# A diffusion layer's latents and context laid out turned by the host, and their reciprocal roots computed on all partitions

## The chip, the cores and the metric

The kernel runs on 1 core of a Trainium2 chip, in one launch. The metric is the device time of one execution in microseconds (us), median of several runs.

Engines are named as in the profile: PE is TensorE (PEld its weight loads), DVE is VectorE, ACT is ScalarE, POOL is GpSimd, SP is SyncE, which here only issues DMAs.

## The reference

One layer of a diffusion backbone over 1024 latent tokens of width 1024, with 256 context tokens. What matters for this change is the very first step, the modulated RMS norm of the latents and of the context:

```python
def rms_norm(x, g):
    xf = x.astype(jnp.float32)
    y = xf * lax.rsqrt(jnp.mean(xf * xf, axis=-1, keepdims=True) + EPS)
    return (y * g.astype(jnp.float32)).astype(x.dtype)
...
    m_lat = sc @ w_mod[l] + b_mod[l]
    m_ctx = scc @ w_mod[l] + b_mod[l]
    ...
    h_lat = rms_norm(x, norm1_g[l]) * (1.0 + sc1) + sh1
    h_ctx = rms_norm(ctx, norm1_g[l]) * (1.0 + csc1) + csh1
    y_lat, y_ctx = token_mixers(h_lat, h_ctx, w_in[l], ...)   # h @ w_in: seven blocks of 512 columns, then retention and differential attention
    x = x + g1 * y_lat
    h2 = rms_norm(x, norm2_g[l]) * (1.0 + sc2) + sh2
    x = x + g2 * conv_ffn(h2, w_up[l], conv_w[l], conv_b[l], w_down[l])
return rms_norm(x, final_g)
```

The products of `h_lat` and `h_ctx` with `w_in` contract over the width, so TensorE needs `h` with the width on the partitions. The mean of squares runs over the same width.

## The kernel before, in words

Every large product is made of three passes over operands split into a rounded high part and a low part (fp32r): high by high, high by low, low by high.

The opening of the kernel works on the latents in two halves of 512 tokens (`xs0`, `xs1`: four tiles of 128 tokens x 1024 each) and on the context in two tiles (`xc`). Tokens lie on the partitions. For each tile:

- `square` (line 542, ACT) sums the squares along the row into one column of `sm`.
- `power` takes the reciprocal root: a DVE multiply and add (line 113), then POOL's `pow` with the exponent -0.5 (line 114), both on 128x1.
- `scale` (line 548, DVE) multiplies the row by it.
- `modulate` then turns four 128x128 pieces on PE (line 554, `ident` is the identity), ACT forms the high part `hT[0]` from PSUM with scale and shift of the modulation (line 557), DVE forms the same unrounded as `tmp` (line 559), and DVE or POOL subtracts to get the low part `hT[1]` (line 561). It runs once for each of the 8 pieces `d` of the width.

The modulation columns `mcol` come from `w_mod` beside it: `mod_load` (DMA), `mod_part` (PE, line 526), `mod_row` (ACT, line 530), `mod_sums` (PE line 536, DVE lines 537 and 538).

`part_products(ts, k)` are the first real products: the block of `w_in` that gives the values of the differential attention, for latent tiles 0 and 1, then 2 and 3, over the contraction piece k = 0 to 7 (lines 598, 600, 604). After the loop over k, tiles 4 and 5 follow with `between(t, k)` after each k (lines 131 to 133 of `passes`), and after this stage tiles 6 and 7 and then the two context tiles by `natural`. From there on `pl` products follow.

`turn_over(n)` are products of ones with ones that nobody reads (line 608).

The order of the stage is written out by hand: `in_order(begin)` makes each of PE, DVE, ACT and SP keep the order in which the instructions stand in the program. POOL is not in that list, but its instructions are issued in the order of the program too. So an instruction that waits holds up all that stands behind it on its engine.

`mhalf` is a 128x32 tile of -0.5, `ones` a 128x128 tile of 1. Pools `ev` and `xp` hold the buffers that the changed code uses.

Of the kernel before, what the change touches and what calls it, by code (L numbers as in the profile page):

```python
# [8 lines left out]
F32 = mybir.dt.float32  # L9
# [13 lines left out]
LC = 256  # L23
NTC = LC // P
LK = LC + L
NKT = LK // P
# [41 lines left out]
def r32(ap):  # L68
    return ap.bitcast(F32)
# [3 lines left out]
def kernel(  # L73
    ctx: ExitStack,
    tc: tile.TileContext,
    x: bass.AP,
    ctxt: bass.AP,
    cols: bass.AP,
# [75 lines left out]
    with ExitStack() as p1:  # L154
# [20 lines left out]
        hT = [[hp.tile([P, KD, 512], F32R, name=f"hT{a}{i}") for i in range(2)] for a in range(2)]  # L175
        xs0 = [xr.tile([P, D], F32, name=f"xs{t}") for t in range(4)]
        cT = []
        sm = hp.tile([P, 16], F32, name="sm")
        mcol = hp.tile([P, KD, 2, 2], F32, name="mcol")
# [331 lines left out]
        with ExitStack() as p0:  # L511
# [27 lines left out]

            def square(xt, col):  # L540
                sq = xp.tile([P, D], BF16, name="sq", bufs=1)
                nc.scalar.activation(sq, xt, AF.Square, accum_out=sm[:, col : col + 1])

            def power(col):
                rsqrt(sm[:, col : col + 1], sm[:, col : col + 1], 1.0 / D, EPS, 1)

            def scale(xt, col, c0=0, c1=D):
                nc.vector.tensor_scalar(out=xt[:, c0:c1], in0=xt[:, c0:c1], scalar1=sm[:, col : col + 1], scalar2=None, op0=ALU.mult)

            def modulate(tiles, d, who, hi, lo):  # L550
                n = len(tiles) * P
                pt = pst.tile([P, 512], F32, name="pt", tag="tr")
                for i, t in enumerate(tiles):
                    nc.tensor.transpose(pt[:, i * P : (i + 1) * P], t[:, d * P : (d + 1) * P], ident)
                sh = mcol[:, d, 0, who : who + 1]
                a = mcol[:, d, 1, who : who + 1]
                nc.scalar.activation(hi, pt[:, :n], AF.Identity, scale=a, bias=sh)
                tmp = xp.tile([P, 512], F32, name="tmp", bufs=2)
                nc.vector.tensor_scalar(out=tmp[:, :n], in0=pt[:, :n], scalar1=a, scalar2=sh, op0=ALU.mult, op1=ALU.add)
                eng = nc.gpsimd if d % 2 and d > 1 else nc.vector  # L560
                eng.tensor_tensor(out=lo, in0=tmp[:, :n], in1=r32(hi), op=ALU.subtract)

            mods, wts, rws = mm_tile("pr").rearrange("p (a b) -> p a b", a=2), {}, {}
            part = [mm_tile("pn") for _ in range(4)]
            sl, raws, xc = [], [], []
            xs1 = [xp.tile([P, D], F32, name=f"xs1_{t}") for t in range(4)]

# [17 lines left out]

            def load_row(t, eng=nc.sync):
                eng.dma_start(out=(xs0 + xs1)[t], in_=x[t * P : (t + 1) * P, :])

            def latents(half, d, t0=0, t1=4):
                modulate((xs0, xs1)[half][t0:t1], d, 0, hT[0][half][:, d, t0 * P : t1 * P], hT[1][half][:, d, t0 * P : t1 * P])  # L590

            def context(d):
                modulate(xc, d, 1, cT[0][:, d, :], cT[1][:, d, :])

            def part_products(ts, k):
                hi, lo = wget(k, 0, 512)
                for t in ts:
                    mm(part[t], lat_lhs(t, k)[0], hi, start=(k == 0), stop=False)
                for t in ts:
                    mm(part[t], lat_lhs(t, k)[0], lo, start=False, stop=False)  # L600
                if k == 0 and 3 in ts:
                    latents(0, 1)
                for t in ts:
                    mm(part[t], lat_lhs(t, k)[1], hi, start=False, stop=(k == KD - 1))

            def turn_over(n):
                for _ in range(n):
                    mm(part[3][:, :P], ones, ones, start=True, stop=True)

            store = store_to(dv_row, c0=NTC)  # L610
            begin = len(nc.cur_bb.bb.instructions)
            mod_load(0, 0, nc.scalar)
            load_row(0, nc.scalar)
            w_load(0, 0, 1, nc.scalar)
            nc.sync.dma_start(out=ident, in_=consts[:, K_ID : K_ID + P])
            load_row(1)
            mod_load(0, 1)
            for t in range(2, 4):
                load_row(t)
            for q in range(2):  # L620
# [5 lines left out]
            nc.vector.tensor_copy(cz[:, :, 0:2], csil)  # L626
            turn_over(9)
            mod_part(0, 0)
            mod_load(2, 1)
            turn_over(9)  # L630
            mod_part(0, 1)
            w_load(1)
            turn_over(2)
            nc.vector.tensor_tensor(out=fold, in0=ident[:, 0:2], in1=ident[:, 32:34], op=ALU.add)
            for g in (64, 96):
                nc.vector.tensor_tensor(out=fold, in0=fold, in1=ident[:, g : g + 2], op=ALU.add)
            square(xs0[0], 2)
            power(2)
            scale(xs0[0], 2, 0, 3 * P)
            square(xs0[1], 3)  # L640
            power(3)
            mod_row(0)
            w_split(0, 1, nc.scalar)
            scale(xs0[1], 3, 0, 3 * P)
            mod_sums(0)
            turn_over(1)
            w_split(0, 1, nc.vector)
            square(xs0[2], 4)
            latents(0, 0, 0, 2)
            square(xs0[3], 5)  # L650
            power(4)
            scale(xs0[0], 2, 3 * P, D)
            power(5)
            scale(xs0[1], 3, 3 * P, D)
            scale(xs0[2], 4, 0, 3 * P)
            scale(xs0[3], 5, 0, 3 * P)
            for q in range(2):
                mod_load(3, q)
            for k in range(KD):
                part_products((0, 1), k)  # L660
                if k == 0:
                    for q in range(2):
                        mod_part(1, q)
                    mod_row(1)
                    latents(0, 0, 2, 4)
                    mod_sums(1)
                    w_split(1, 2)
                if k == 1:
                    mod_sums(2)
                    latents(0, 2)  # L670
                    for t in (2, 3):
                        scale(xs0[t], 2 + t, 3 * P, D)
                    for q in range(2):
                        mod_part(3, q)
                    mod_row(3)
                if k == 4:
                    square(xs1[2], 8)
                    power(8)
                    scale(xs1[0], 6)
                if k == 5:  # L680
                    scale(xs1[2], 8)
                    scale(xs1[3], 9)
                if k >= 6:
                    latents(1, 4 * (k - 6))
                    latents(1, 4 * (k - 6) + 1)
                if 0 < k < 5:
                    load_row(k + 3)
                n = k + 4
# [17 lines left out]
                if k in (0, 2, 4):  # L706
                    w_split()
                if k == 3:
                    square(xs1[0], 6)
                    square(xs1[1], 7)  # L710
                    power(6)
                    power(7)
                if k == 4:
                    scale(xs1[1], 7)
                    square(xs1[3], 9)
                    power(9)
                if k == 5:
                    first.close()
                    cp = pctx.enter_context(tc.tile_pool(name="cp", bufs=1, side="right"))
                    cT.extend(cp.tile([P, KD, LC], F32R, name=f"cT{a}") for a in range(2))  # L720
                    for t in range(NTC):
                        xc.append(xp.tile([P, D], F32, name="xc", tag="wt", bufs=5))
                        nc.sync.dma_start(out=xc[t], in_=ctxt[t * P : (t + 1) * P, :])
                if k >= 6:
                    latents(1, 4 * (k - 6) + 2)
                    latents(1, 4 * (k - 6) + 3)
            rtab = load_rope(1)
            for t in range(2):
                store(t, part[t])

            def between(t, k):
                if (t, k) == (4, 1):
                    for i in (2, 3):
                        store(i, part[i])
                if t == 4 and k in (3, 5):
                    i = (k - 3) // 2
                    square(xc[i], i)
                    power(i)
                if t == 4 and k in (5, 7):
                    i = (k - 5) // 2  # L740
                    scale(xc[i], i)
                if t == 5 and k % 2:
                    context(k - 1)
                    context(k)

# [844 lines left out]
def lay_out(inputs):  # L1590
# [16 lines left out]
    def kmajor(w, nb):  # L1607
# [8 lines left out]
        "x": a["x"][0],  # L1616
        "ctxt": a["ctx"][0],
        "cols": cols,
# [25 lines left out]
```

## Time and profile before

| | |
|---|---|
| median of 3 runs | 1389.49 us (1388.88 to 1389.71) |
| profiled execution | 1387.15 us, of which the span is 1385.4 us |
| mean granted TensorE clock | 0.998 |
| PE busy | 1363.2 us, 98% of the span |
| DVE, ACT, POOL busy | 994.4, 732.2, 303.6 us |

The span is what the profiler saw between the first and the last instruction. In lists by line or tile, a row gives the engine, the operation, the tiles written and read (`out<-in`), shapes, the count and then durations; three numbers with strokes are the least, the median and the most in ns. In a timeline a row begins with its start and its length in us; a product of plain f32 stands there as two records.

### The profile page before, as it was taken

To read this page: it belongs to the slowest core of one execution; us is meant where nothing else is said; L and a number is where in the kernel's file an instruction comes from. 1 tells how busy PE (TensorE), PEld (TensorE's weight loads), DVE (VectorE), ACT (ScalarE), POOL (GpSimd) and SP (SyncE) were. 2 spreads that over 40 slices of the span, in tenths; PEclk is the share of its full clock that TensorE was granted. 3 is DMA by queue.
4 is the path that set the end of the run, shared out by engine and by line. 5 is a ranking of instruction groups with operands and counts; after the bars stand their busy time and mean duration, and the time that the engine had idled before them with its cause. 6 is when DMAs were issued, how large, how long until landed. Compare 5 with 4: busy or idle time off the path is not lost. (4 is left out here: it accounts for less than half of the span.)

```text
span 1385.4 us, 19442 instructions
## 1 busy us (share of the span) xinstructions
PE 1363.2 (98%) x7042; PEld 1146.0 (83%) x7042; DVE 994.4 (72%) x1469; ACT 732.2 (53%) x1395; POOL 303.6 (22%) x323
## 2 busy tenths in 40 slices
PE   8999999999999999999999999999999999999997
PEld 6788888888988799998888788888888888888886
DVE  4655773424676898895458997788778877798757
ACT  4652322434675789987136654555545555454543
POOL 1310000002655424411200643222332220000001
PEclk9999999999999999999999999999999999999999
DMA  9546885454565778622410232332323325963523
GB/s 373 202 168 210 296 267 184 145 176 144 155 188 151 208 179 182 139 48 99 172 65 23 99 115 99 114 114 94 112 101 112 113 71 174 373 227 106 175 92 129
DMA packets 94759, 214.61 MB, mean 155 GB/s; under 512 B 9220, under 2 KB 29188, under 8 KB 94152
## 3 DMA queue, kind: packets, MB, share of 16 engines
q1 hardware_dynamic: 85928, 186.90, 39.2%
q0 software_dynamic: 8160, 24.91, 7.9%
q10 hardware_dynamic: 576, 1.57, 0.3%
q8 instruction: 55, 0.90, 0.3%
q14 instruction: 40, 0.33, 0.1%
HBM read 158.03 MB, written 55.31 MB: 154 GB/s over the span
## 5 line engine op out<-in xcount | busy, mean ns | idle before, releaser
L131 PE MATMUL pl<-hT,whi 128*128 128x512 f32 x256 | 105.8, 413 | 0.0
L131 PE MATMUL chain<-T,whi 128*128 128x512 f32 x264 | 103.0, 391 | 1.2 <-ACT ub L1298 0.9
L132 PE MATMUL chain<-T,whi 128*128 128x512 f32 x264 | 102.8, 389 | 0.0
L133 PE MATMUL chain<-T,wlo 128*128 128x512 f32 x264 | 102.4, 389 | 0.0
L133 PE MATMUL pl<-hT,wlo 128*128 128x512 f32 x256 | 100.2, 391 | 0.0
L132 PE MATMUL pl<-hT,whi 128*128 128x512 f32 x256 | 99.9, 390 | 0.0
L876 DVE TENSOR_REDUCE mt<-pA 128x1 f32<-128x1280 f32 x64 | 95.1, 1489 | 3.0 <-PE pA L873 1.3
L873 PE MATMUL pA<-ks,qhl 128*128 128x512 f32 (+1 forms) x384 | 89.5, 369 | 1.4 <-DMA ks<-dk 1.0
L131 PE MATMUL c<-whi,ghl 128*128 128x512 f32 x232 | 90.2, 389 | 0.0
L132 PE MATMUL c<-wlo,ghl 128*128 128x512 f32 x232 | 90.2, 389 | 0.0
L133 PE MATMUL c<-whi,ghl 128*128 128x512 f32 x232 | 90.2, 389 | 0.0
L880 ACT ACTIVATE p<-pA,mt 128x1280 f32<-128x1280 f32 x64 | 85.5, 1336 | 5.5 <-DVE mt L876 5.4
L1044 ACT CAST whi<-cmb 128x512 fp32r<-128x512 f32 x62 | 38.5, 623 | 80.5 <-PE chain L132 66.3
L873 PEld LDWEIGHTS pA<-ks,qhl 128*128 128x128 f32 x384 | 67.7, 189 | 13.8 <-issue 1.4
L905 PE MATMUL pv<-va,aT 128*128 128x128 f32 x640 | 77.0, 275 | 0.1
L1204 POOL TENSOR_TENSOR cmb<-wrb 128x512 f32<-128x512 f32 x19 | 28.3, 1488 | 221.1 <-DMA wrb<-w_up 168.2
L1047 DVE TENSOR_TENSOR wlo<-cmb,whi 128x512 fp32r<-128x512 f32 x62 | 60.0, 970 | 20.4 <-ACT whi L1044 20.4
L905 PEld LDWEIGHTS pv<-va,aT 128*128 128x128 f32 x640 | 73.9, 192 | 0.7 <-DVE yT L934 0.3
L1044 ACT CAST whi<-wra 128x512 fp32r<-128x512 f32 x55 | 33.9, 623 | 72.9 <-PE third L132 42.3
L133 PE MATMUL third<-yT,wlo 128*128 128x512 f32 x168 | 65.4, 389 | 0.0
L132 PE MATMUL third<-yT,whi 128*128 128x512 f32 x168 | 65.4, 389 | 0.0
L131 PE MATMUL third<-yT,whi 128*128 128x512 f32 x168 | 65.4, 389 | 0.0
(327 smaller groups left out, 3843.0 us busy)
## 6 DMA issues: line engine op xcount, KB each, us to landing
wm<-w_mod SPq DMA_DIRECT2D x32, 512.0 KB, 5.1
raw<-w_in SPq DMA_DIRECT2D x27, 512.0 KB, 4.7
wra<-w_up SPq DMA_DIRECT2D x24, 512.0 KB, 3.3
wrb<-w_up SPq DMA_DIRECT2D x22, 512.0 KB, 3.5
W<-w_down SPq DMA_DIRECT2D x44, 256.0 KB, 5.8
ad<-s SPq DMA_DIRECT2D x20, 512.0 KB, 3.6
wra<-ad SPq DMA_DIRECT2D x20, 512.0 KB, 3.7
kvs<-kvg SPq DMA_DIRECT2D x36, 256.0 KB, 3.1
```

The source lines that it names most:

```text
L131: mm(ps, lh, rh, start=first, stop=False, skip_group_check=more)
L132: mm(ps, lh, rl, start=False, stop=False, skip_group_check=more)
L133: return mm(ps, ll, rh, start=False, stop=last, skip_group_check=more)
L873: mm(self.pa[m][:, c0:c1], self.q[:, m, i, qs], self.k[:, m, c0:c1], start=(i == 0), stop=(i == 1))
L876: nc.vector.tensor_reduce(out=self.mt[:, m : m + 1], in_=self.pa[m][:, :LK], axis=AX.X, op=ALU.min)
L880: nc.scalar.activation(self.p[m], self.pa[m][:, :LK], AF.Exp, scale=-1.0, bias=self.mt[:, m : m + 1], accum_out=self.s[:, m : m + 1])
L905: mm(self.pv, self.aT[:, c, :], self.v[:, c, :], start=(c == 0), stop=(c == NKT - 1))
L1044: cast = nc.scalar.copy(hi, src)
L1047: nc.vector.tensor_tensor(out=lo, in0=src, in1=r32(hi), op=ALU.subtract)
L1204: nc.gpsimd.tensor_tensor(out=s1, in0=b1, in1=b2, op=ALU.add)
```

## The change

The host turns x and the context: the new input `xt` holds, for each of five groups of 256 tokens (four of latents, the fifth the context), the width on the partitions as [128, 8, 256]. The context no longer comes as an input of its own.

```diff
-        xs0 = [xr.tile([P, D], F32, name=f"xs{t}") for t in range(4)]
+        xh = [xr.tile([P, 2, KD, GQ], F32, name="xh0")]        # GQ = 256
...
+            def x_load(g, i, eng=nc.sync):
+                dst = xc[i] if g == 4 else xh[g // 2][:, g % 2, 4 * i : 4 * i + 4, :]
+                eng.dma_start(out=dst, in_=xt[g][:, 4 * i : 4 * i + 4, :])
+
+            def squares(g, k0, k1):
+                ...
+                nc.scalar.activation(sqs[g, i][:, k0 % 4 : k0 % 4 + k1 - k0, :], src, AF.Square)
+
+            def summed(g, i):
+                ...
+                nc.vector.tensor_reduce(out=sums[g][:, i, :], in_=sqs[g, i].rearrange("p k q -> p q k"), axis=AX.X, op=ALU.add)
+
+            def over_rows(g, srcs, first, last):
+                if first:
+                    tot[g] = pst.tile([P, GQ], F32, name="ss", tag="tr")
+                for n, src in enumerate(srcs):
+                    mm(tot[g], ones, src, start=first and n == 0, stop=last and n == len(srcs) - 1)
+
+            def rstd(g):
+                r = Rc if g == 4 else R[g // 2][:, g % 2, :]
+                nc.vector.tensor_scalar(out=r, in0=tot[g], scalar1=1.0 / D, scalar2=EPS, op0=ALU.mult, op1=ALU.add)
+                nc.gpsimd.tensor_tensor(out=r, in0=r, in1=mhalf[:, 0:1].to_broadcast([P, GQ]), op=ALU.pow)
+
+            def modulate(src, r, d, who, hi, lo):
+                n = hi.shape[-1]
                 sh = mcol[:, d, 0, who : who + 1]
                 a = mcol[:, d, 1, who : who + 1]
-                nc.scalar.activation(hi, pt[:, :n], AF.Identity, scale=a, bias=sh)
-                tmp = xp.tile([P, 512], F32, name="tmp", bufs=2)
-                nc.vector.tensor_scalar(out=tmp[:, :n], in0=pt[:, :n], scalar1=a, scalar2=sh, op0=ALU.mult, op1=ALU.add)
-                eng = nc.gpsimd if d % 2 and d > 1 else nc.vector
-                eng.tensor_tensor(out=lo, in0=tmp[:, :n], in1=r32(hi), op=ALU.subtract)
+                u = xp.tile([P, 512], F32, name="u", bufs=2)[:, :n]
+                nc.vector.scalar_tensor_tensor(out=u..., in0=src, scalar=a, in1=r, op0=ALU.mult, op1=ALU.mult)
+                nc.scalar.activation(hi, u, AF.Identity, bias=sh)
+                nc.vector.scalar_tensor_tensor(out=lo, in0=u, scalar=sh, in1=r32(hi), op0=ALU.add, op1=ALU.subtract)
+
+            def latents(half, d, g0=0, g1=2): ...      # modulate for groups g0 to g1 of a half
+            def context(d): ...                        # modulate for the context, with Rc
+            def first_latents(): ...                   # piece 0 of group 0: u = x * R on DVE, then hi on ACT, u and lo on DVE
```

The order of the stage, new lines marked (loads of weights and modulations left out):

```diff
+            x_load(0, 1, nc.scalar)
             mod_load(0, 0, nc.scalar)
+            x_load(0, 0)
             ...
+            turn_over(11)
+            for k in (0, 2, 4, 6):
+                squares(0, k, k + 2)
+            for k in (0, 2, 4):
+                over_rows(0, [sqs[0, k // 4][:, k % 4 + e, :] for e in range(2)], k == 0, False)
             mod_part(0, 0)
+            over_rows(0, [sqs[0, 1][:, 2 + e, :] for e in range(2)], False, True)
+            mod_part(0, 1)
             ...
+            rstd(0)
+            opening = first_latents()
+            next(opening)
             mod_row(0)
             w_split(0, 1, nc.scalar)
+            turn_over(1)
             mod_sums(0)
+            next(opening)
             w_split(0, 1, nc.vector)
             ...
             for k in range(KD):
                 part_products((0, 1), k)
                 if k == 0:
+                    for e in range(0, KD, 2):
+                        squares(1, e, e + 2)
+                    for i in range(2):
+                        over_rows(1, [sqs[1, i][:, e, :] for e in range(4)], i == 0, i == 1)
                     for q in range(2):
                         mod_part(1, q)
+                    rstd(1)
+                    latents(0, 0, 1, 2)
                     mod_row(1)
                     mod_sums(1)
                     w_split(1, 2)
+                    latents(0, 1)
                 ...
                 if k == 4:
+                    squares(2, 0, 4)
+                    summed(2, 0)
                 if k == 5:
+                    over_rows(2, [sums[2][:, i, :] for i in range(2)], True, True)
+                    rstd(2)
+                if k == 7:
+                    squares(3, 4, 8)
+                    summed(3, 0)
                 if k >= 6:
+                    latents(1, 3 * k - 16, 0, 1)
+                    if k == 7:
+                        summed(3, 1)
+                    latents(1, 3 * k - 15, 0, 1)
                 ...
                 part_products((2, 3), k)
                 ...
                 if k == 4:
+                    squares(2, 4, 8)
+                    summed(2, 1)
                 if k == 5:
                     ...
+                    latents(1, 0, 0, 1)
+                    latents(1, 1, 0, 1)
                 if k >= 6:
+                    latents(1, 3 * k - 14, 0, 1)
+                if k == 6:
+                    squares(3, 0, 4)
...
+            over_rows(3, [sums[3][:, i, :] for i in range(2)], True, True)
+            rstd(3)
             def between(t, k):
                 ...
+                if t == 4:
+                    latents(1, k, 1, 2)
+                    if k in (3, 5):
+                        squares(4, 2 * k - 6, 2 * k - 2)
+                    if k == 7:
+                        for i in range(2):
+                            summed(4, i)
+                if t == 5:
+                    if k == 0:
+                        over_rows(4, [sums[4][:, i, :] for i in range(2)], True, True)
+                        rstd(4)
+                    else:
+                        context(k - 1)
+                    if k == 7:
+                        context(k)
...
-        "ctxt": a["ctx"][0],
+        "xt": np.concatenate([a["x"][0], a["ctx"][0]]).T.reshape(KD, P, -1, GQ).transpose(2, 1, 0, 3),
```

Gone are `square`, `power`, `scale`, the old `modulate` with its turns, and `load_row`.

More of the change, by code (lines that the diff above doesn't have):

```diff
@@ L24 @@
 NTC = LC // P
+GQ = 256
 LK = LC + L
@@ L76 @@
     x: bass.AP,
-    ctxt: bass.AP,
+    xt: bass.AP,
     cols: bass.AP,
@@ L175 @@
         hT = [[hp.tile([P, KD, 512], F32R, name=f"hT{a}{i}") for i in range(2)] for a in range(2)]
-        xs0 = [xr.tile([P, D], F32, name=f"xs{t}") for t in range(4)]
+        xh = [xr.tile([P, 2, KD, GQ], F32, name="xh0")]
         cT = []
-        sm = hp.tile([P, 16], F32, name="sm")
+        pad(hp, 64)
         mcol = hp.tile([P, KD, 2, 2], F32, name="mcol")
@@ L538, in mod_sums @@
                 nc.vector.tensor_scalar(out=mcol[:, d, 0, :], in0=pm[:, 0, :], scalar1=cl[:, COL_BMOD + d : COL_BMOD + d + 1], scalar2=None, op0=ALU.add)
[L540 to L554, printed above, removed]
+            def x_load(g, i, eng=nc.sync):
+                dst = xc[i] if g == 4 else xh[g // 2][:, g % 2, 4 * i : 4 * i + 4, :]
+                eng.dma_start(out=dst, in_=xt[g][:, 4 * i : 4 * i + 4, :])
@@ new lines, in squares @@
+            def squares(g, k0, k1):
+                i = k0 // 4
+                if k0 % 4 == 0:
+                    sqs[g, i] = ev.tile([P, 4, GQ], F32, name="sq", tag="xhl")
+                src = xc[i][:, k0 % 4 : k0 % 4 + k1 - k0, :] if g == 4 else xh[g // 2][:, g % 2, k0:k1, :]
+                nc.scalar.activation(sqs[g, i][:, k0 % 4 : k0 % 4 + k1 - k0, :], src, AF.Square)
+            def summed(g, i):
+                if i == 0:
+                    sums[g] = ev.tile([P, 2, GQ], F32, name="sqk", tag="xb")
+                nc.vector.tensor_reduce(out=sums[g][:, i, :], in_=sqs[g, i].rearrange("p k q -> p q k"), axis=AX.X, op=ALU.add)
@@ L561, in modulate, with latents @@
-                eng.tensor_tensor(out=lo, in0=tmp[:, :n], in1=r32(hi), op=ALU.subtract)
+                u = xp.tile([P, 512], F32, name="u", bufs=2)[:, :n]
+                nc.vector.scalar_tensor_tensor(out=u.rearrange("p (g q) -> p g q", q=GQ), in0=src, scalar=a, in1=r, op0=ALU.mult, op1=ALU.mult)
+                nc.scalar.activation(hi, u, AF.Identity, bias=sh)
+                nc.vector.scalar_tensor_tensor(out=lo, in0=u, scalar=sh, in1=r32(hi), op0=ALU.add, op1=ALU.subtract)
+            def latents(half, d, g0=0, g1=2):
+                c = slice(g0 * GQ, g1 * GQ)
+                modulate(xh[half][:, g0:g1, d, :], R[half][:, g0:g1, :], d, 0, hT[0][half][:, d, c], hT[1][half][:, d, c])
@@ new lines, in context, with first_latents @@
+            def context(d):
+                modulate(xc[d // 4][:, d % 4 : d % 4 + 1, :], Rc.unsqueeze(1), d, 1, cT[0][:, d, :], cT[1][:, d, :])
+            def first_latents():
+                sh = mcol[:, 0, 0, 0:1]
+                a = mcol[:, 0, 1, 0:1]
+                hi, lo = (hT[i][0][:, 0, 0:GQ] for i in range(2))
+                u = xp.tile([P, 512], F32, name="u", bufs=2)[:, :GQ]
+                nc.vector.tensor_tensor(out=u, in0=xh[0][:, 0, 0, :], in1=R[0][:, 0, :], op=ALU.mult)
+                yield
+                nc.scalar.activation(hi, u, AF.Identity, scale=a, bias=sh)
+                nc.vector.tensor_scalar(out=u, in0=u, scalar1=a, scalar2=sh, op0=ALU.mult, op1=ALU.add)
+                nc.vector.tensor_tensor(out=lo, in0=u, in1=r32(hi), op=ALU.subtract)
+                yield
@@ L565 @@
             sl, raws, xc = [], [], []
-            xs1 = [xp.tile([P, D], F32, name=f"xs1_{t}") for t in range(4)]
+            xh.append(xp.tile([P, 2, KD, GQ], F32, name="xh1"))
+            R = [xp.tile([P, 2, GQ], F32, name=f"R{i}") for i in range(2)]
+            Rc = xp.tile([P, GQ], F32, name="Rc")
+            sqs, sums, tot = {}, {}, {}
             def wget(k, c0, c1):
@@ L584, in w_split @@
                     nc.vector.tensor_tensor(out=lo, in0=raw, in1=r32(hi), op=ALU.subtract)
[L586 to L593, printed above, removed]
             def part_products(ts, k):
@@ L600, in part_products @@
                     mm(part[t], lat_lhs(t, k)[0], lo, start=False, stop=False)
-                if k == 0 and 3 in ts:
-                    latents(0, 1)
                 for t in ts:
@@ L611 @@
             begin = len(nc.cur_bb.bb.instructions)
+            x_load(0, 1, nc.scalar)
             mod_load(0, 0, nc.scalar)
-            load_row(0, nc.scalar)
-            w_load(0, 0, 1, nc.scalar)
+            x_load(0, 0)
+            mod_load(0, 1)
             nc.sync.dma_start(out=ident, in_=consts[:, K_ID : K_ID + P])
[L616 to L619, printed above, removed]
+            w_load(0, 0, 1)
+            for i in range(2):
+                x_load(1, i)
             for q in range(2):
@@ L626 @@
             nc.vector.tensor_copy(cz[:, :, 0:2], csil)
-            turn_over(9)
+            turn_over(11)
[3 more added lines that the diff above has]
+                over_rows(0, [sqs[0, k // 4][:, k % 4 + e, :] for e in range(2)], k == 0, False)
             mod_part(0, 0)
+            over_rows(0, [sqs[0, 1][:, 2 + e, :] for e in range(2)], False, True)
+            mod_part(0, 1)
             mod_load(2, 1)
-            turn_over(9)
-            mod_part(0, 1)
             w_load(1)
-            turn_over(2)
             nc.vector.tensor_tensor(out=fold, in0=ident[:, 0:2], in1=ident[:, 32:34], op=ALU.add)
@@ L636 @@
                 nc.vector.tensor_tensor(out=fold, in0=fold, in1=ident[:, g : g + 2], op=ALU.add)
[L637 to L641, printed above, removed]
+            rstd(0)
+            opening = first_latents()
+            next(opening)
             mod_row(0)
             w_split(0, 1, nc.scalar)
-            scale(xs0[1], 3, 0, 3 * P)
+            turn_over(1)
             mod_sums(0)
-            turn_over(1)
+            next(opening)
             w_split(0, 1, nc.vector)
[L648 to L656, printed above, removed]
             for q in range(2):
@@ L661 @@
                 if k == 0:
+                    for e in range(0, KD, 2):
+                        squares(1, e, e + 2)
+                    for i in range(2):
+                        over_rows(1, [sqs[1, i][:, e, :] for e in range(4)], i == 0, i == 1)
                     for q in range(2):
                         mod_part(1, q)
+                    rstd(1)
+                    latents(0, 0, 1, 2)
                     mod_row(1)
-                    latents(0, 0, 2, 4)
                     mod_sums(1)
                     w_split(1, 2)
+                    latents(0, 1)
                 if k == 1:
@@ L670 @@
                     latents(0, 2)
-                    for t in (2, 3):
-                        scale(xs0[t], 2 + t, 3 * P, D)
                     for q in range(2):
@@ L676 @@
                 if k == 4:
-                    square(xs1[2], 8)
-                    power(8)
-                    scale(xs1[0], 6)
+                    squares(2, 0, 4)
+                    summed(2, 0)
                 if k == 5:
-                    scale(xs1[2], 8)
-                    scale(xs1[3], 9)
+                    over_rows(2, [sums[2][:, i, :] for i in range(2)], True, True)
[3 more added lines that the diff above has]
+                    summed(3, 0)
                 if k >= 6:
-                    latents(1, 4 * (k - 6))
-                    latents(1, 4 * (k - 6) + 1)
+                    latents(1, 3 * k - 16, 0, 1)
+                    if k == 7:
+                        summed(3, 1)
+                    latents(1, 3 * k - 15, 0, 1)
                 if 0 < k < 5:
-                    load_row(k + 3)
+                    x_load(2 + (k - 1) // 2, (k - 1) % 2)
                 n = k + 4
@@ L707 @@
                     w_split()
[L708 to L712, printed above, removed]
                 if k == 4:
-                    scale(xs1[1], 7)
-                    square(xs1[3], 9)
-                    power(9)
+                    squares(2, 4, 8)
+                    summed(2, 1)
                 if k == 5:
@@ L720 @@
                     cT.extend(cp.tile([P, KD, LC], F32R, name=f"cT{a}") for a in range(2))
-                    for t in range(NTC):
-                        xc.append(xp.tile([P, D], F32, name="xc", tag="wt", bufs=5))
-                        nc.sync.dma_start(out=xc[t], in_=ctxt[t * P : (t + 1) * P, :])
+                    for i in range(2):
+                        xc.append(xp.tile([P, 4, GQ], F32, name="xc", tag="wt", bufs=5))
+                        x_load(4, i)
+                    latents(1, 0, 0, 1)
+                    latents(1, 1, 0, 1)
                 if k >= 6:
-                    latents(1, 4 * (k - 6) + 2)
-                    latents(1, 4 * (k - 6) + 3)
+                    latents(1, 3 * k - 14, 0, 1)
+                if k == 6:
+                    squares(3, 0, 4)
             rtab = load_rope(1)
@@ L734, in between @@
                         store(i, part[i])
[L735 to L744, printed above, removed]
+                if t == 4:
[3 more added lines that the diff above has]
+                    if k == 7:
+                        for i in range(2):
+                            summed(4, i)
[7 more added lines that the diff above has]
+                        context(k)
             for t in (4, 5):
```

## The prediction

> **What bounds the kernel now.** I read the engines' totals first, then the table by stage of the opening, which is all that the diff touches.
>
> ```profile
> span 1385.4 us, 19442 instructions
> PE 1363.2 (98%) x7042; PEld 1146.0 (83%) x7042; DVE 994.4 (72%) x1469; ACT 732.2 (53%) x1395; POOL 303.6 (22%) x323
> ...
> 0.00:13.50 13.50, 8.79 (x65) 7.31 (x65) 3.40 (x18) 6.25 (x12) 1.63 (x7) 1.00 0.85 312
> 13.50:58.30 44.80, 42.54 (x297) 30.13 (x298) 30.79 (x59) 22.59 (x37) 9.52 (x10) 1.00 0.82 322
> 58.30:82.10 23.80, 23.80 (x114) 19.33 (x113) 13.73 (x28) 13.80 (x24) 8.37 (x10) 1.00 0.23 87
> 82.10:93.00 10.90, 10.90 (x50) 9.01 (x48) 6.77 (x35) 6.00 (x21) 0.00 (x0) 1.00 0.73 290
> ```
>
> Columns after the length are busy us of PE, PEld, DVE, ACT, POOL. PE is full from 13.5 us on but for 2.3 us, so the end moves by whatever moves PE's stream. The timeline gives the marks that I compare with:
>
> ```profile
> 13.50 0.73 PE L598 MATMUL pn<-whi,hT 128*128 128x512 f32 x2 [0.87 <-ACT hT L557]
> 17.56 0.73 PE L598 MATMUL pn<-whi,hT 128*128 128x512 f32 x2 [0.18 <-ACT hT L557]
> 42.65 0.74 PE L598 MATMUL pn<-whi,hT 128*128 128x512 f32 x2
> 58.34 0.47 PE L131 MATMUL pn<-whi,hT 128*128 128x512 f32 x1
> 82.34 0.39 PE L131 MATMUL pn<-whi,cT 128*128 128x512 f32 x1
> 93.22 0.39 PE L131 MATMUL pl<-hT,whi 128*128 128x512 f32 x1
> ```
>
> They are: first product (k = 0, tiles 0 and 1); k = 0, tiles 2 and 3; start of k = 5; tile 4; context; the first product after all that the diff touches. The context's 48 products take 93.22 - 82.34 = 10.88 us, 0.227 each. The forecast is the new time of the last mark.
>
> **The price that decides: pow on 256 columns.** Before, POOL raised one column at a time, in one place four:
>
> ```profile
> L114 POOL TENSOR_TENSOR sm<-sm,mhalf x18: 550/555/1043, 8.8 to 744.5; 128x1 f32<-128x1 f32 x18
> L273 POOL TENSOR_TENSOR ss<-ss,mhalf x16: 1011/1017/1483, 340.8 to 434.6; 128x4 f32<-128x4 f32 x16
> ...
> 340.81 1.02 POOL L273 TENSOR_TENSOR ss<-ss,mhalf 128x4 f32<-128x4 f32 x1 [1.33 <-ACT ss L272]
> 341.86 1.14 DVE L278 SCALAR_TENSOR_TENSOR o<-o,ss,gn 128x128 f32<-128x128 f32 x4 [1.27 <-POOL ss L273]
> ...
> L916 POOL TENSOR_TENSOR e<-sa 128x1 f32<-128x1 f32 x32 | 6.0, 192 | 0.2
> L561 POOL TENSOR_TENSOR hT<-tmp,hT 128x512 fp32r<-128x512 f32 x6 | 7.7, 1292 | 31.6 <-DVE tmp L559 31.6
> L561 POOL TENSOR_TENSOR cT<-tmp,cT 128x256 fp32r<-128x256 f32 x3 | 2.2, 737 | 7.4 <-DVE tmp L559 7.4
> ```
>
> The page calls POOL's spans rough, but the reader of the four columns starts 0.03 us after the shown end, so this length is real. Three more columns cost 1017 - 555 = 462 ns, 154 ns each, while a subtraction costs (1292 - 737) / 256 = 2.2 ns per column. At 154 ns a pow of 256 columns takes X = 0.555 + 255 x 0.154 = 39.8 us, and there are five (four latent groups and the context). No row shows more than 4 columns. The bounds: from below the subtraction's 2.2 ns, X = 1.1 us; from above the longest four columns, (1483 - 555) / 3 = 309 ns, X = 79 us. That one is a straggler (the median of 16 lies 6 ns above the least), so the range ends lower, at a fifth over the median. I take 154 ns: same operation, engine and type, medians of 34 executions. That work has been replicated 128-fold (every partition raises the same numbers) does not help, since the columns are what costs.
>
> By the Trainium skill (GPSIMD Engine Reference, § 3.1) a two-input elementwise instruction there costs about 2.6 cycles per element of a row at 1.2 GHz. The subtraction's row agrees (2.2 ns); the pow rows do not. By that rule each pow would be an estimate of about 1 us and the sum that of the first rival. The same page's § 2.1 describes the instruction as a loop over the elements in which each core serves its 16 partitions, which is what a cost by the column looks like.
>
> **The other prices.**
>
> ```profile
> 7.35 1.06 ACT L542 ACTIVATE sq<-xs 128x1024 bf16<-128x1024 f32 x1 [1.99 <-DMA xs<-x]
> ...
> L582 ACT CAST whi<-raw x5: 610/1052/1058, 11.3 to 44.1; 128x1024 fp32r<-128x1024 f32 x3, 128x512 fp32r<-128x512 f32 x2
> ...
> L537 DVE TENSOR_SCALAR mcol<-pm,bsc,cl 128x2 f32<-128x2 f32 x8 | 2.2, 276 | 3.9 <-PE pm L536 3.9
> L538 DVE TENSOR_SCALAR mcol<-pm,cl 128x2 f32<-128x2 f32 x8 | 1.7, 211 | 0.0
> L561 DVE TENSOR_TENSOR hT<-tmp,hT 128x256 fp32r<-128x256 f32 x2 | 0.8, 424 | 0.1
> L584 DVE TENSOR_TENSOR wlo<-raw,whi 128x512 fp32r<-128x512 f32 x2 | 1.4, 682 | 0.0
> L406 DVE TENSOR_REDUCE mu<-st 128x4 f32<-128x512 f32 x10 | 6.8, 683 | 9.6 <-ACT st L403 9.6
> ...
> 148.29 1.88 PE L494 MATMUL pg<-macc,ones 128*128 128x512 f32 x4
> 31.53 0.64 PE L554 MATMUL pt<-ident,xs 128*128 128x128 f32 x4
> 32.09 1.07 PE L526 MATMUL pr<-wt,cz 128*32 128x256 f32 x16
> ```
>
> ACT over SBUF: 0.61 us for 512 columns, 1.05 for 1024, so 0.40 for 256. DVE with two inputs: 0.42 for 256; `summed` 1.2 (0.68 for 512, doubled less the start). A plain f32 product over 512 columns takes 0.94 us (1.88 for two), so 0.45 over 256: 22 of them are 9.9 us. Four turns take 32.09 - 31.53 = 0.56 us, so the 80 that go are 11.2. PE's own work thus changes by 1.3 us only. One `latents` of 256 columns is now a chain, u on DVE (0.42), hi on ACT (0.40), lo on DVE (0.42), with some 0.04 us at each of three handovers 1.35 us; lo stands behind u in DVE's order and the next u behind lo, so successive pieces don't overlap. POOL's share of the lows moves to DVE.
>
> **The sum.** Every pow is waited for by a u at the head of DVE's queue. Behind it stand all later DVE work, behind the hi on ACT the squares of the next group, and the next `over_rows` on PE needs those squares. So the five pows run one after another, and the path is:
>
> - a, start to pow 0: the first x tile was there at 7.35 us; 2 x 512 KB of x now head two queues, so I keep 7.0. Four squares 2.5, two last products and the modulation part between 1.1, multiply and add 0.4: 11.0.
> - b, to pow 1: u 0.42, `mcol` 0.49, hi 0.5, u again, lo and `wlo` 1.6 (DVE), four products, then eight `over_rows` 3.6 and 0.4; with handovers 7.6.
> - c, to pow 2: u and hi 0.9, then tiles 2 and 3 of k = 0 through tiles 0 and 1 of k = 5. Before: 17.56 to 42.65 + 6 x 0.227 = 44.0, 26.5 us, less six sets of four turns (3.4) and some 1.2 of waits: 21.9. Two `over_rows` 0.9, 0.4: 24.2.
> - d, to pow 3: five pieces 6.8, squares and sums up to the second sum 4.4, two `over_rows` 0.9, two pieces that stand ahead on DVE and the multiply and add 2.1: 14.2.
> - e, to pow 4: eight pieces 10.8, squares between them 0.4, two sums 2.4, `over_rows` and DVE 1.4: 15.0.
> - f, to the end of the context's products: eight pieces 10.8, three passes 0.7, second tile 5.5: 17.0.
>
> Together 89.0. One term more: PE stands still for 40 us at a time.
>
> ```profile
> 1.20 3.66 PE L608 MATMUL pn<-ones 128*128 128x128 f32 x18 [1.20 <-DVE ones L110]
> ...
> 6.27 2.27 PE L608 MATMUL pn<-ones 128*128 128x128 f32 x18
> ```
>
> The same 18 records take 3.66 us at the start and 2.27 later, 1.4 us lost on a cold PE, though the granted clock reads 1.00 in both. PE's products follow a pow directly in b, c and f: 3 x 1.4 = 4.2. The Trainium skill (TensorE: Matmul & The Clock Gate, § What's actually happening) has PE back at half clock after an idle window of about 3.4 us, and full after as long a busy one. The start agrees; no row before shows a long pause in mid-run. Without the effect the sum is 4.2 us less.
>
> New mark: 89.0 + 4.2 + 5 x 39.8 = 292.2 us against 93.2, so +199.0. After it nothing changes. The span becomes 1584.4, the profiled execution 1387.15 + 199.0 = 1586.2; the median shown is 2.3 above that execution, so 1389.49 + 199.0 = 1588.5. Since 89.0 + 4.2 is what the stage took before, the change costs 5X as long as X decides.
>
> **The rivals.**
>
> 1. Pow costs per column like the subtraction, X = 1.1. For it: 256 columns could be looped better than four. Against: the four columns. Then PE sets the pace: first product at 13.5 as now; tiles 2 and 3 at 22.1 (eight `over_rows` and pow 1 lie between), k = 5 done near 43.5 with turns and waits gone, tile 4 at 58. But pow 3 starts at 61.3 and pow 4's sums need 14.6 us more: PE, in order, stands at `over_rows(4)` in tile 5 from 64 to 75, and the mark falls at 102.5: +9.3, 1399.
> 2. Long pows overlap their columns in part, X between 3 and 23. By 5X that is +15 to +115: 1405 to 1505. No row speaks for it, none excludes it.
> 3. The other side: faster. TensorE is the only bound, the roots are as cheap as the subtraction, and the waits of rival 1 vanish because pieces overlap. From 13.5 on PE then loses 11.2 of turns and 2.3 of idle, and gains 14 `over_rows`, 6.3: -7.2, 1382. It decides only with X under about 1 us and the handovers hidden; above 2.7 us (where 89.0 + 5X passes rival 1's 102.5) no cover is left.
>
> **How the numbers follow.** Forecast 0.82, rival 1 0.06, rival 2 0.08, rival 3 0.04. A measurement can tell some 0.2% from no change, 2.8 us. Slower 0.95, same 0.01, faster 0.04. The forecast's own range: X from 29 us (three quarters of the slope) to 47, with 10 us for the path, 1525 to 1635. Carried to the top of rival 2 and a little of the longer rows above: 1505 to 1640; what lies outside is the rest of rival 2, rivals 1 and 3, and X over 50.
>
> **What would show it.** Right: five POOL instructions 128x256 near 40 us each, one after another; PE busy near 30% of the first 290 us; waits of DVE's u for POOL's pow near 200 us in total; the first `pl` product near 292 us; products at half speed after a pause. Wrong: a pow under 10 us, pows beside PE work, or the first `pl` product before 110 us.

## The result: 1609.94 us, 16% slower

The changed kernel takes 1609.94 us (median of 4 runs, 1608.08 to 1611.3) against 1389.6 us beside it: a ratio of 1.1584, interval 1.1564 to 1.1604, or +220.3 us. The prediction was 1588.5 us (+199.0), range 1505 to 1640. The profiled execution took 1611.3 us; its page begins so (busy us by engine; further down the granted clock and POOL's busy share over 40 slices, and the costliest group):

```profile
span 1609.5 us, 19313 instructions
PE 1380.8 (86%) x6988; PEld 1153.3 (72%) x6988; DVE 1008.1 (63%) x1483; ACT 732.2 (45%) x1397; POOL 490.9 (31%) x309
...
PE   3226114499999999999999999999999999999997
...
POOL 5774595500000066542511204433222222000001
PEclk6558557799999999999999999999999999999999
...
L566 POOL TENSOR_TENSOR R<-R,mhalf 128x256 f32<-128x256 f32 x4 | 164.5, 41128 | 76.7 <-DVE R L565 76.7
```

All that is new lies in the first eight slices, where POOL is the busy engine and PE works a third of the time (103 of the first 316 us). POOL's own timeline names it:

```profile
16.62 41.15 POOL L566 TENSOR_TENSOR R<-R,mhalf 128x256 f32<-128x256 f32 x1 [15.57 <-DVE R L565]
68.44 41.13 POOL L566 TENSOR_TENSOR R<-R,mhalf 128x256 f32<-128x256 f32 x1 [10.68 <-DVE R L565]
143.70 41.12 POOL L566 TENSOR_TENSOR R<-R,mhalf 128x256 f32<-128x256 f32 x1 [34.13 <-DVE R L565]
201.16 41.12 POOL L566 TENSOR_TENSOR R<-R,mhalf 128x256 f32<-128x256 f32 x1 [16.34 <-DVE R L565]
259.08 41.12 POOL L566 TENSOR_TENSOR Rc<-Rc,mhalf 128x256 f32<-128x256 f32 x1 [16.80 <-DVE Rc L565]
```

Five pows of 41.1 us, none beside another, each begun only when DVE hands over the next sum; from the second on, the idle time before a pow (in brackets) is the path between two of them. Who waited longest in the first 330 us, and the marks that the prediction used, on PE:

```profile
DVE u L573 <- POOL R L566: 120.1, 3, 41.2
...
DVE u L589 <- POOL R L566: 41.3, 1, 41.3
DVE u L573 <- POOL Rc L566: 41.2, 1, 41.2
...
59.22 1.22 PE L625 MATMUL pn<-whi,hT 128*128 128x512 f32 x2 [41.48 <-ACT hT L591]
111.82 1.20 PE L625 MATMUL pn<-whi,hT 128*128 128x512 f32 x2
198.55 0.99 PE L132 MATMUL pn<-whi,hT 128*128 128x512 f32 x1
301.31 0.79 PE L132 MATMUL pn<-whi,cT 128*128 128x512 f32 x1 [37.97 <-ACT cT L574]
315.79 0.39 PE L132 MATMUL pl<-hT,whi 128*128 128x512 f32 x1
```

DVE stood 202.6 us for POOL. The last mark, the first `pl` product, moved from 93.2 to 315.8 us: +222.6 of the span's +224.1. Behind it only 1.5 us were added.

### The profile page after: what moved, and what is told of

The parts are those of the page before. It is cut to its first block, busy times and chain, and to the rows that moved or that the text cites. A ratio compares the mean times of both kernels' runs of the same rounds, so it can differ in the third digit from the quotient of the medians.

```text
span 1609.5 us, 19313 instructions
## 1 busy us (share of the span) xinstructions
PE 1380.8 (86%) x6988; PEld 1153.3 (72%) x6988; DVE 1008.1 (63%) x1483; ACT 732.2 (45%) x1397; POOL 490.9 (31%) x309
## 3 DMA queue, kind: packets, MB, share of 16 engines
q1 hardware_dynamic: 86072, 187.16, 34.1%
## 5 line engine op out<-in xcount | busy, mean ns | idle before, releaser
L566 POOL TENSOR_TENSOR R<-R,mhalf 128x256 f32<-128x256 f32 x4 | 164.5, 41128 | 76.7 <-DVE R L565 76.7
L132 PE MATMUL pn<-whi,hT 128*128 128x512 f32 x160 | 66.2, 419 | 36.5 <-ACT hT L574 36.5
L573 DVE SCALAR_TENSOR_TENSOR u<-xh,mcol,R 128x256 f32<-128x256 f32 (+1 forms) x24 | 13.3, 556 | 120.1 <-POOL R L566 120.1
L574 ACT ACTIVATE hT<-u,mcol 128x256 fp32r<-128x256 f32 (+1 forms) x24 | 13.7, 571 | 162.1 <-DVE u L573 162.1
```

The lines of the kernel that those rows point to most:

```text
L132: mm(ps, lh, rh, start=first, stop=False, skip_group_check=more)
L566: nc.gpsimd.tensor_tensor(out=r, in0=r, in1=mhalf[:, 0:1].to_broadcast([P, GQ]), op=ALU.pow)
L574: nc.scalar.activation(hi, u, AF.Identity, bias=sh)
```

## The experiments

**The pow taken out (e1).** `rstd` multiplies instead:

```diff
-nc.gpsimd.tensor_tensor(out=r, in0=r, in1=mhalf[:, 0:1].to_broadcast([P, GQ]), op=ALU.pow)
+nc.gpsimd.tensor_tensor(out=r, in0=r, in1=mhalf[:, 0:1].to_broadcast([P, GQ]), op=ALU.mult)
```

> The changed kernel with POOL multiplying by -0.5 where it raised to the power -0.5; the reciprocal root is left out. If the loss is the five pows in a row (41.1 us each), each falls to about 0.8 us, PE has no long pauses and stays warm: 5 x 40.3 = 202 us and some 12 us of slow clock go, about 1397 us, near the first rival's 1399. If the loss lay in the rest of the new chain (squares, products with ones, pieces of 256 columns), it stays above 1450 us. If the third rival's picture of the rest is right, it ends near 1382.

1411.6 us, ratio 1.0167 (1.0152 to 1.0182). Same shape, same operands, same place:

```profile
16.27 0.61 POOL L566 TENSOR_TENSOR R<-R,mhalf 128x256 f32<-128x256 f32 x1 [15.22 <-DVE R L565]
26.91 0.61 POOL L566 TENSOR_TENSOR R<-R,mhalf 128x256 f32<-128x256 f32 x1 [10.02 <-DVE R L565]
...
18.53 0.73 PE L625 MATMUL pn<-whi,hT 128*128 128x512 f32 x2 [1.13 <-ACT hT L591]
29.36 0.70 PE L625 MATMUL pn<-whi,hT 128*128 128x512 f32 x2
77.53 0.99 PE L132 MATMUL pn<-whi,hT 128*128 128x512 f32 x1
104.35 0.39 PE L132 MATMUL pn<-whi,cT 128*128 128x512 f32 x1
116.46 0.39 PE L132 MATMUL pl<-hT,whi 128*128 128x512 f32 x1
```

198 of the 220 us go with the operation alone. But 23 stay, where 8 were expected: what is left of the change is slower than the turns it replaced, by more than the first rival had it, and the third rival (1382) is out.

**A quarter of the columns (e2).** `rstd` raises `r[:, :64]` only.

> The changed kernel with pow on 64 of each 256 columns; the other 192 are left without their root. By the column (41.12 - 1.02 over 252 columns is 159 ns): 0.555 + 63 x 0.159 = 10.6 us per pow, five times 30.5 us less than 1610, so 1457 us. If a long pow were cheaper per column than a short one (a fixed part in the 41 us), more than 11 us per pow and over 1460 us.

1457.64 us (one execution), 0.6 from the expectation. Pow and last mark:

```profile
15.14 10.54 POOL L566 TENSOR_TENSOR R<-R,mhalf 128x64 f32<-128x64 f32 x1 [14.10 <-DVE R L565]
...
161.15 0.39 PE L132 MATMUL pl<-hT,whi 128*128 128x512 f32 x1
```

From 64 to 256 columns the pow grows by 30.6 us, 159 ns per column, the same as from 4 to 64 (10.54 - 1.02 over 60: 159). Long pows are no cheaper by the column than short ones, so the second rival falls. The mark moves by 315.79 - 161.15 = 154.6 us, 1.01 of five times 30.6: every us of every pow is paid in full. Of the 1.6 us above, 1.5 are chance rather than pow: the first pow starts at 15.14 us here and at 16.62 in the changed kernel, with the same instructions before it.

**PE kept busy in the pauses (e3).** `filler(n)` issues n products of ones with ones into a PSUM tile of its own.

```diff
-            turn_over(11)
+            turn_over(22)
...
+filler(150) after mod_sums(0); filler(150) before rstd(1); filler(165) before over_rows(3); filler(130) at the end of tile 4
```

> The changed kernel with products of ones that nobody reads put into PE's pauses (22 instead of 11 at the start, 150, 150, 165 and 130 in the first four pauses), each set shorter than the pause. If PE running at half clock after the pauses is what the path lost beside the pows (path 110 us without the pows against 89 worked out), some 10 to 13 us go: about 1598. By the prediction's 1.4 us after each of three pauses only 4 go: 1606. If the products delay what follows, slower than 1610.

1617.77 us (one execution), slower. The trace shows a warm opening and pauses that were filled only in part:

```profile
8.66 2.86 PE L561 MATMUL ss<-sq,ones 128*128 128x256 f32 x12
13.69 41.15 POOL L566 TENSOR_TENSOR R<-R,mhalf 128x256 f32<-128x256 f32 x1 [12.64 <-DVE R L565]
254.74 41.12 POOL L566 TENSOR_TENSOR Rc<-Rc,mhalf 128x256 f32<-128x256 f32 x1 [17.18 <-DVE Rc L565]
...
313.48 0.39 PE L132 MATMUL pl<-hT,whi 128*128 128x512 f32 x1
321.73 0.80 PE L132 MATMUL pl<-hT,whi 128*128 128x512 f32 x1 [5.38 <-ACT whi L188]
...
56.30 1.22 PE L625 MATMUL pn<-whi,hT 128*128 128x512 f32 x2 [7.88 <-ACT hT L591]
106.91 1.01 PE L537 MATMUL pm<-fold,rw 128*128 128x2 f32 x4 [8.35 <-ACT rw L531]
```

In the opening PE is warm: the first pow starts 2.9 us earlier. The last pow starts 4.3 us earlier and the mark falls 2.3 us earlier. Then PE waits 5.4 us for the weights of the next block, whose split now stands late on ACT, which more than takes this back; the span ends 6.5 us later, and what else adds to that lies further on. But the fillers end 7.6 to 20.2 us before PE goes on, and the products behind the first two pauses take as long as in the changed kernel (1.22 us; granted clock 0.50 from 106 to 112 us). So the 4.3 us are mostly the opening's. What half clock behind the pauses costs, this run does not show.

**Pow on two columns (e4).** The squares become the weights and ones the data, so that 128 tokens lie on the partitions and pow has one column for each 128; the identity times the roots is multiplied by ones to spread them.

```diff
-mm(tot[g], ones, src, ...)
+for c in range(2):
+    mm(tot[g][:, c, :], src[:, c * P : (c + 1) * P], ones[:, 0:2], ...)
...
+def spread(g):     # dg = ident * root per token, pr = ones^T dg, R = pr
```

> The full computation: the sums of squares are made with the squares as weights and ones as data, so that 128 tokens lie on the partitions, pow runs on 2 columns (about 0.7 us by the rows for 1 and 4), the identity times the roots is multiplied by ones and so spread over the partitions. About 2.5 us per group in place of 41.1: 1400 to 1405 if the rest of the chain is what the multiplication alone leaves. Under 1389 if the pieces of 256 hide, above 1420 if the detour over PE holds up its order.

1423.38 us, ratio 1.0249 (1.0231 to 1.0266). As written it probably leaves a part of each sum of squares out (no run shows which), so only its time is read.

```profile
16.50 0.71 POOL L567 TENSOR_TENSOR root<-root,mhalf 128x2 f32<-128x2 f32 x1 [15.45 <-DVE root L566]
...
73.82 1.01 PE L575 MATMUL pR<-dg,ones 128*128 128x128 f32 x4 [2.90 <-DVE dg L573]
```

The pow is 0.71 us, as the rows for 1 and 4 columns said, yet the run takes 12 us more than e1. The row shows a part of it: the root of this group is ready at 68.83 us, but `dg` comes on DVE only at 73.49, behind other work, and the spread, which stands in PE's order, waits 2.9 us for it. The rest of the 12 us is not taken apart.

**Two remedies on e1 (root left out), one at a time.** e5 has `turn_over(22)` for 11. In e6 each lo is issued behind the next piece's u.

> The kernel that multiplies in place of pow (root left out, 1411.6 us), with 22 instead of 11 unread products of ones at the start, so that PE is not idle between 6.3 and 8.5 us. If the half clock in the opening (over_rows 0.46 us dearer each, first product at 18.5 against 13.5 us before) is part of the 23 us that are left without pow, pow's place starts near 13.4 instead of 16.3 us and the first pl product comes some 3 to 4 us earlier than 116.5: 1408. If waits for modulation weights and for DVE's sums later on absorb it: 1411.

1409.91 us (one execution). The mark comes at 112.28 us, 4.2 earlier, the end only 1.7 earlier.

> The kernel that multiplies in place of pow (root left out, 1411.6 us), with each lo of the second half and of the context put behind the next piece's u on DVE, so that DVE does not stand during hi. A piece takes 1.46 us now; DVE's share is about 0.85. If the pieces of 256 columns bound the stretch from 64 to 115 us, some 0.4 us go per piece on 6 + 8 + 8 pieces, 6 to 9 us: 1403 to 1406. If DVE's reductions (1.9 us each) and PE's order bound it, under 2 us: 1410.

1405.48 us (one execution). The mark comes at 110.52, 5.9 earlier; 1.1 of that was there at the first product already (17.41 us), which the edit doesn't touch. DVE rows of the changed kernel, then of e8, which has the same edit:

```profile
242.31 0.48 DVE L573 SCALAR_TENSOR_TENSOR u<-xh,mcol,R 128x256 f32<-128x256 f32 x1 [41.23 <-POOL R L566]
243.37 0.49 DVE L575 SCALAR_TENSOR_TENSOR hT<-u,mcol,hT 128x256 fp32r<-128x256 f32 x1 [0.58 <-ACT hT L574]
243.77 0.48 DVE L573 SCALAR_TENSOR_TENSOR u<-xh,mcol,R 128x256 f32<-128x256 f32 x1
```

```profile
84.74 0.49 DVE L581 SCALAR_TENSOR_TENSOR u<-xh,mcol,R 128x256 f32<-128x256 f32 x1
85.14 0.48 DVE L584 SCALAR_TENSOR_TENSOR hT<-u,mcol,hT 128x256 fp32r<-128x256 f32 x1
85.66 0.49 DVE L581 SCALAR_TENSOR_TENSOR u<-xh,mcol,R 128x256 f32<-128x256 f32 x1
```

From u to u 1.46 us as changed, with 0.58 of standing still; 0.92 us in e8.

**The root elsewhere, the computation whole (e7).**

```diff
-nc.gpsimd.tensor_tensor(out=r, in0=r, in1=mhalf[:, 0:1].to_broadcast([P, GQ]), op=ALU.pow)
+nc.scalar.activation(r, r, AF.Sqrt)
+nc.vector.reciprocal(r, r)
```

> The full computation of the changed kernel with the root by ACT (Sqrt) and DVE (reciprocal) on the 256 columns in place of POOL's pow. ACT takes 0.4 to 0.5 us by its rows, the reciprocal between 0.4 us (as a subtraction) and 2 us, a table load 1.3 us once or twice: X between 1 and 2.6 us against 41.1. If the five serial pows are the loss and the rest is what the multiplication showed, 1413 to 1422 us; well under 200 us of the 220 gone would mean that pow's place, not its price, was wrong.

1416.49 us, ratio 1.0188 (1.0172 to 1.0203).

```profile
L567 DVE RECIPROCAL R<-R 128x256 f32<-128x256 f32 x4 | 7.0, 1753 | 1.9 <-ACT R L566 1.9
L566 ACT ACTIVATE R<-R 128x256 f32<-128x256 f32 x4 | 1.7, 417 | 14.0 <-DVE R L565 14.0
```

0.42 + 1.75 us in place of 41.1, and 193 of the 220 us are back, with the same layout, the same products with ones and the same order. The price of pow was the loss, not its place.

**With the remedies (e8, e9).** e8 adds the edits of e5 and e6 to e7; e9 also sums by additions:

```diff
-nc.vector.tensor_reduce(out=sums[g][:, i, :], in_=sqs[g, i].rearrange("p k q -> p q k"), axis=AX.X, op=ALU.add)
+nc.vector.tensor_tensor(out=sq[:, 0:2, :], in0=sq[:, 0:2, :], in1=sq[:, 2:4, :], op=ALU.add)
+nc.vector.tensor_tensor(out=sums[g][:, i, :], in0=sq[:, 0, :], in1=sq[:, 1, :], op=ALU.add)
```

> The full computation: root by ACT and DVE, 22 products at the start, and each lo behind the next u. If both remedies add to the one before, about 10 us under it: 1403 to 1411. To beat the kernel before (1388) the pieces, the sums and the opening would all have to hide, as the third rival had it.

> The full computation with the root by ACT and DVE, the warm start and each lo behind the next u (1410.5 us), and each of the six DVE reductions (1.92 us, four slices 256 apart) replaced by two additions of neighbouring slices (0.69 + 0.42 us by the subtraction's rows). If the sums stand on the path of the groups 2, 3 and 4, as worked out (one in c, two each in d and e), 0.8 us go five times: 1406 to 1407. If PE's order or the pieces hide them, 1410.

e8 1410.53 us, ratio 1.0142 (1.0125 to 1.0159); e9 1407.8 us, 1.0135 (1.0116 to 1.0155). Two DVE rows of e9 against one of the changed kernel:

```profile
L556 DVE TENSOR_TENSOR sq<-sq 128x512 f32<-128x512 f32 x6 | 4.1, 687 | 1.9 <-ACT sq L550 1.9
L557 DVE TENSOR_TENSOR sqk<-sq 128x256 f32<-128x256 f32 x6 | 2.6, 426 | 0.2
```

```profile
L555 DVE TENSOR_REDUCE sqk<-sq 128x256 f32<-128x1024 f32 x6 | 11.4, 1918 | 0.9 <-ACT sq L550 0.9
```

1.11 us a sum instead of 1.92. The intervals of e8 and e9 overlap; the 2.7 us between the medians are of the size expected, the mark comes 4.2 us earlier (113.38 to 109.23), and no more is claimed. No version here beats the kernel before. Where the rest lies, by the marks of PE (us):

| mark | before | e1 | e9 |
|---|---|---|---|
| first product | 13.50 | 18.53 | 17.18 |
| k = 0, tiles 2 and 3 | 17.56 | 29.36 | 29.77 |
| k = 5 | 42.65 | 53.01 | 55.01 |
| tile 4 | 58.34 | 77.53 | 74.05 |
| context | 82.34 | 104.35 | 98.36 |
| first `pl` | 93.22 | 116.46 | 109.23 |

Twelve us of e9's sixteen are lost before k = 0 is through: before, tiles 2 and 3 follow the first 4 us later, now eight plain f32 products, a root and a piece lie between. The loop over k wins nothing back though its turns are gone.

## Why the prediction was right, term by term

**The price of pow.** Taken from the rows for 1 and 4 columns, 39.8 us; measured 41.1. The slope was right to 3% over a stretch of 64 times the length. Five times 1.3 us is 6.6 of the 23.6 us by which the mark came later than forecast. By the rule of the Trainium skill (GPSIMD Engine Reference, § 3.1, about 2.6 cycles per element) e1's multiplication is in place (0.61 us, against an estimate from that figure of 0.55 for 256 elements, plus a start); the pow takes some seventy times that estimate. That section of the Trainium skill gives no price for a pow.

**The five in a row.** Right: e2 shows every pow paid in full, and the timeline shows how the next one hangs on the last. After pow 0 come, one behind the other, u on DVE, hi on ACT (58.57 us), the squares of the next group behind it on ACT (59.08), their sums on PE and the multiply and add on DVE:

```profile
57.80 0.42 DVE L589 TENSOR_TENSOR u<-xh,R 128x256 f32<-128x256 f32 x1 [41.26 <-POOL R L566]
62.61 5.29 PE L561 MATMUL ss<-sq,ones 128*128 128x256 f32 x16
67.94 0.42 DVE L565 TENSOR_SCALAR R<-ss 128x256 f32<-128x256 f32 x1 [7.26 <-PE ss L561]
```

That they would be as dear in another order is not shown, and no run tries one. POOL alone would still need 5 x 41.1 = 205.6 us for them; hiding all that lies between the pows (b to e below) could save 78 us at the most, an estimate.

**The path between them.** Mis-sized: 110.2 us with the slow clock in it, against 89.0 + 4.2. From the starts and ends of the pows in POOL's timeline (c's own terms in the forecast add up to 24.1):

| | forecast | measured |
|---|---|---|
| a, to pow 0 | 11.0 | 16.6 |
| b | 7.6 | 10.7 |
| c | 24.2 | 34.1 |
| d | 14.2 | 16.3 |
| e | 15.0 | 16.8 |
| f, to the first `pl` | 17.0 | 15.6 |

In a and b about half of the miss is the f32 products on a cold PE. In a twelve records take 2.86 us when warm (e3) and 5.49 here, and a is 13.7 us in e3; how cold it is varies (4.25 us for the twelve in e2). In b sixteen take 5.29 us, where the warm rate would give 3.8. The slow-clock term put 1.4 us behind each of three pows and nothing into a, where I had no pause. That its 4.2 us come near the 4.3 that e3 gives back is luck: e3's gain is mostly a's. By these rows and the difference between c here and in e1 (34.1 and 31.6) the clock costs about 2.6 us in a, 1.5 in b and 2.5 in c; that makes some 7 us, an estimate, so the term was too small.

In d and e it is mostly `summed`, twice each 1.92 us where I took 1.2 from a reduction over neighbouring elements. The largest is c:

```profile
8.61 5.49 PE L561 MATMUL ss<-sq,ones 128*128 128x256 f32 x12 [3.10 <-ACT sq L550]
...
135.79 0.64 PE L527 MATMUL pr<-wt,cz 128*32 128x256 f32 x8 [0.73 <-DMA wt<-w_mod]
137.00 0.64 PE L527 MATMUL pr<-wt,cz 128*32 128x256 f32 x8 [0.57 <-DMA wt<-w_mod]
140.23 1.02 PE L561 MATMUL ss<-sqk,ones 128*128 128x256 f32 x2
142.21 0.70 PE L561 MATMUL ss<-sqk,ones 128*128 128x256 f32 x2 [0.96 <-DVE sqk L555]
...
109.00:115.00 6.00, 4.05 (x14) 2.88 (x18) 3.18 (x7) 2.01 (x4) 0.57 (x1) 0.50 0.00 0
...
127.00:133.00 6.00, 6.00 (x46) 4.29 (x39) 3.78 (x7) 3.07 (x6) 0.00 (x0) 1.00 1.03 402
```

(In the last two rows, by stage, the three figures at the end are granted clock, DMA share and GB/s.) Of c's 9.9 us, 1.4 lie before tiles 2 and 3 of k = 0 (111.82 us, 2.25 after the pow, where I had 0.9), 6.5 from there to `over_rows` (28.4 us against 21.9) and 2.2 behind that, 0.96 of them a wait for `summed`. e1, without the long pause, needs 25.1 us for the middle stretch (29.36 to 54.50), so half clock is about 3.3 of the 6.5 (e1's c as a whole is only 2.5 shorter, since its PE then waits 2.55 us for `summed`); 1.3 are the two waits for modulation weights in the rows, and 2 I cannot place.

I had carried the old pace of the loop over, with its loads in time. In the pauses almost nothing is loaded (26 GB/s from 69 to 109.5 us), because the buffers are full and their readers wait (SP stands up to 51.4 us at a time until PE has read a `wt`); when PE goes on, the loads run at 402 GB/s. But the pauses are not what makes PE wait for weights: e1 waits there for 1.2 us as well. The Trainium skill (TensorE: Matmul & The Clock Gate, § What's actually happening) says half clock after an idle window: the granted clock of 0.50 right after pow 1 agrees, and so does e3, where 8.4 us of idle were enough for 0.50.

**The first rival's 1399** was 13 us short of e1. Its mechanism was wrong too: PE does not stand at `over_rows(4)`, because products of tiles 6 and 7 are issued ahead of it; e1's trace shows 0.39 us of wait there (97.16 us). Its loss was not there but in the opening (11.8 of the 23.2 us at the second mark of the table), and, by e6 and e9, in the pieces and the sums.

## What to carry to other kernels

An operation's price per element must be read from two sizes of its own rows, not from another operation on the same engine: 1 and 4 columns sufficed to forecast 256. Moving a reduced value from one column per tile to a full row on all partitions multiplies the work on it by the tokens of a tile; where the operation on it is slow, reduce, take the root small, or take it on another engine. An order written out by hand can turn such a price into a wait for every engine behind it; here it counted in full each of the five times.

## What was not expected of the hardware

POOL multiplies 256 columns by a broadcast column in 0.61 us, less than the 0.74 us of its subtraction of two full operands, or the 0.77 of a multiplication of two (line 282 of e1, 16 times). DVE's reciprocal over 256 columns takes 1.75 us, over four times a multiplication of that size (0.42). A reduction over four elements that lie 256 apart takes 1.92 us for 1024 elements, where two additions of the same data take 1.11.
